# Turning update factors and probabilities on VectorE, GpSimd and ScalarE, and queueing VectorE's side work behind the weight splits, in a hybrid attention/RWKV layer on one core

## The chip, the core and the metric

One core of a Trainium2 chip runs the whole layer in one launch. The metric is the device time of that launch in microseconds (us). Its engines are TensorE (PE in the profile; its weight loads are PEld), VectorE (DVE), ScalarE (ACT), GpSimd (POOL) and SyncE (SP), which here issues nearly all DMAs. Each engine works through its own list of instructions in order; an instruction that waits holds back all behind it on that engine.

## What is computed

The reference, cut to what matters here (shapes: 256 tokens, width 4096, 16 FoX heads of 128, 32 RWKV heads of 64, chunks of 64):

```python
def reference(x, w_in, f_bias, mu_shift, w0, w_up, a0, a_up, k_k, k_a, r_k, gn_gain, gn_bias, w_out, ln_gain, ln_bias):
    proj = jnp.einsum('bsd,dc->bsc', x, w_in)
    ...
    fox_out = _fox_attention(fq, fk, fv, log_f)
    ...
    rw = rw + (rw_prev - rw) * mu_shift
    r, kr, vr, wd, ad = jnp.split(rw, _split_points(IN_SIZES[4:9]), axis=-1)
    w_raw = -jax.nn.softplus(-(w0 + jnp.tanh(wd) @ w_up)) - 0.5
    decay = jnp.exp(-jnp.exp(w_raw))
    a = jax.nn.sigmoid(a0 + ad @ a_up)
    ...
    y = _rwkv7_scan(rh, decay, kh, vh, -kk, kk * ah)
    ...
    h = jnp.concatenate([fox_out, rwkv_out], axis=-1) * jax.nn.silu(z)
    out = jnp.einsum('bsc,cd->bsd', h, w_out)
    return _layernorm(ALPHA * x + out, ln_gain, ln_bias, LN_EPS)
```

In `_fox_attention` a block of 128 queries takes the softmax of its logits (a score plus a decay bias, causal) and multiplies the probabilities with the values. `_rwkv7_scan` is the recurrence `S = S diag(w) + (S a) b^T + v k^T; y = S r`, frame by frame.

## The kernel before

**Main work.** The input projection runs as 8 head pairs (n) of 4 blocks (b) of 512 columns, each over 4096 rows in 16 pieces (q) of 128x1024 weights; the output projection as 8 blocks of the same pieces. A piece is called w{n}_{b}_{q} (w4_3_13 is piece 13 of block 3 of pair 4; the profile leaves the pair and block out and calls it w_13). Every weight is split in a high and a low part: ScalarE writes the high one (L141), VectorE the rest (L142, the "split"). A piece then takes 12 matmuls of 512 columns on TensorE (L147 to L149; L880 to L882 for the output), of which four read the low part, the first of them third in order. `weights` keeps three pieces traced ahead: while TensorE works on piece q, the split last traced (`latest`) is that of piece q+2. The low parts have three buffers, so the split of piece q+2 can start when TensorE has ended piece q-1; the high parts have four.

**Side work.** All the rest (the heads' attention and recurrence, and the way from projection to heads) is cut into generators. `slot()` is called after each 6 matmuls, twice a piece, and moves every generator one `yield` on; so `wait(W[...])` puts steps a number of slots apart. `W` is a table of such distances. What a slot traces comes after the main work traced before it in priority, but a scheduler orders each engine's list: an instruction whose inputs are there may go ahead of earlier traced ones that still wait. Only the side work inside `with behind(...)` (the SV steps of pair 0 and the first softmax step of heads 0 and 1) is tied to come after the split last traced.

- `prepare` and `front` (L419, L471) make, for each 128 channels i, the decays. They split the low-rank weights upt into uph (ScalarE) and upl (VectorE, L424); one slot later six small matmuls (lp, L430 to L432) read both.
- `rwkv` (L522) treats a pair in chunks of 64. It makes the gram products gp, scales the update factors BK on GpSimd (L538), and turns BK for all four chunks with TensorE into tp (L571) and copies it to BKt with ScalarE (L572). Then it solves a triangular system row by row: 31 rows, each one multiply (L600) and one reduction (L603) on VectorE, one row a slot. Then come vm (L615) and eight SV steps (L623), and, some 12 slots on, the state update: rh, up and sp on TensorE with copies between. sp (L687) reads BKt, for chunks 0 to 2 only. The solved rows go through DRAM (td, T) to the matmuls qt (L638).
- `fox` (L734) does one head: the scores fsp (L743, L744), the softmax steps lg (L750 to L754, the exponential on ScalarE), three transposes of the probabilities on TensorE (fpt, L758), a ScalarE copy to pT (L760), and `W["fo"]` = 3 slots later the product with the values fop (L764, L765). Head 2n's softmax falls in block 3 of pair n, head 2n+1's in the pair after.
- `unload` turns each finished block on VectorE (bk, L809) and sends it through DRAM.

Of the kernel before, what the change touches and what calls it, by code (L numbers as in the profile page):

```python
# [10 lines left out]
F32 = mybir.dt.float32  # L11
# [3 lines left out]
ALU = mybir.AluOpType  # L15
AX = mybir.AxisListType

P = 128
# [4 lines left out]
C = 64  # L23
NCH = S // C
HD = 64
LORA = 96
NF = 16
# [17 lines left out]
BEHIND = 13  # L45
W = {"fo": 3, "vs": 2, "np": 4, "gp": 5, "tp": 4, "d1": 8, "d2": 12, "xp": 3, "fs": 4, "fp": 5}
NB = D // OB
# [3 lines left out]
B = 32  # L51
# [33 lines left out]
def layer(ctx: ExitStack, tc: tile.TileContext, xt, xtok, w_main, w_lora, w_first, muv, w_o, up, par, mulora, fbias, lng, lnb, cst, out):  # L85
    nc = tc.nc
# [8 lines left out]
    def pst(name):  # L95
        return ps.tile([P, 512], F32, tag="ps", name=name)
# [34 lines left out]
    ident = cs[:, C_ID : C_ID + P]  # L131
# [4 lines left out]
    latest = [None]  # L136
# [50 lines left out]

    def behind(first):
        return tc.issue_after(latest[0].ins) if first else nullcontext()

    sides = []
# [8 lines left out]
    def slot():  # L200
        for g in list(sides):
            try:
                next(g)
            except StopIteration:
                sides.remove(g)

# [56 lines left out]
    rp = mid.enter_context(tc.tile_pool(name="rp", bufs=1))  # L263
# [65 lines left out]
    ct = const.tile([P, 2 * NF], F32, name="ct")  # L329
# [69 lines left out]
    def flat(t):  # L399
        return t.rearrange("p a b -> p (a b)")  # L400
# [121 lines left out]
    def rwkv(n):  # L522
# [4 lines left out]
        lc, BK, LT, bon = q["lc"], q["BK"], q["lt"], q["bon"]  # L527
# [3 lines left out]
        for u in range(2):  # L531
            for c in range(NCH):
                for j in range(2):
                    h = HALF[j]
# [31 lines left out]
        yield from wait(W["tp"])  # L566
        BKt = rp.tile([P, 2, NCH, P], F32, tag="shl", name=f"BKt{n}")
        for u in range(2):
            tp = pst(f"tp{n}_{u}")
            for c in range(NCH):  # L570
                nc.tensor.transpose(tp[:, c * P : (c + 1) * P], BK[:, u, c, :], ident)  # L571
            nc.scalar.copy(flat(BKt[:, u]), tp)  # L572
        yield from wait(W["d1"])

# [42 lines left out]
        for j in range(2):  # L617
            o = HALF[1 - j]
            for c in range(2):
                h = HALF[c]  # L620
                for a in range(2):
                    with behind(not n):
                        nc.vector.scalar_tensor_tensor(  # L623
                            SV[j][o, :, 2 * a + c, :], vm[h, a, :, j].unsqueeze(2).to_broadcast([C, 2, HD]), -1.0 / HD, vt[h, a, :, j, :], ALU.mult, ALU.add
                        )
            tc.keep_in_program_order(nc.scalar.copy(UV[j][o], SV[j][o]))
            nc.gpsimd.memset(SV[j][HALF[j], :, 0, :], 0.0)
# [106 lines left out]
    def fox(i, q, k, vt):  # L734
# [13 lines left out]
        for m, blk in enumerate((slice(0, 1), slice(1, 3))):  # L748
            with behind(i < 2):
                nc.vector.scalar_tensor_tensor(lg[:, blk, :], spv[:, blk, :], ct[:, m * NF + i : m * NF + i + 1], nb[:, blk, :], ALU.add, ALU.add)  # L750
            nc.vector.tensor_reduce(st[:, m : m + 1], lg[:, blk, :], AX.XY, ALU.max, negate=True)
            nc.scalar.activation(lg[:, blk, :], lg[:, blk, :], AF.Exp, bias=st[:, m : m + 1], accum_out=st[:, 2 + m : 3 + m])
            nc.vector.reciprocal(st[:, 4 + m : 5 + m], st[:, 2 + m : 3 + m])
            nc.vector.tensor_scalar(lg[:, blk, :], lg[:, blk, :], st[:, 4 + m : 5 + m], None, ALU.mult)  # L754
        yield from wait(W["fp"])
        pt = pst(f"fpt{i}")
        for m in range(3):
            nc.tensor.transpose(pt[:, m * P : (m + 1) * P], lg[:, m, :], ident)  # L758
        pT = rp.tile([P, 3 * P], F32, tag="nb", name=f"pT{i}")
        nc.scalar.copy(pT, pt[:, : 3 * P])  # L760
        yield from wait(W["fo"])
# [145 lines left out]
    vt = None  # L907
# [210 lines left out]
```

## Time and profile before

| | |
|---|---|
| median of 3 runs | 1936.33 us (1934.52 to 1938.71) |
| profiled execution, its own time | 1935.4 us |
| its span | 1933.6 us |
| granted TensorE clock | 0.999 |
| TensorE transposes of BK (L571) | 64 in 8 groups |
| TensorE transposes of probabilities (L758) | 48 in 16 groups |
| VectorE splits of main pieces (L142) | 31 of each of the 16 numbers q, 1.21 to 1.33 us each |
| GpSimd copies (L462) | 96 |

How to read it: a row of the timeline has start, duration, engine, line, operation, the tiles written and read (out<-in) and their shapes; a row of the groups has count, then busy us and mean ns of one, then idle time before it and what ended it; a row of one line has minimum, median and maximum in ns. A row of the waits has who waited, for whom, the total in us, how many times and the longest. The ends of matmuls are modelled, so their distance from start to start tells more than their duration.

### The profile page before, as it was taken

The numbers are of one execution on the slowest core, as the hardware profiler recorded it, in microseconds if no ns is written. First come the engines' busy times: TensorE is split into PE (matmuls) and PEld (weight loads), VectorE is DVE, ScalarE is ACT, GpSimd is POOL, SyncE is SP. The second block draws the span as 40 slices with busy tenths as digits, with TensorE's granted clock in tenths as the row PEclk, the third lists the DMA queues.
The fourth block names the chain that finished last, engine by engine and source line by source line (L and its number), as shares of the span: only waits on it lengthen the run. The fifth ranks groups of instructions, "written<-read, shape, count | busy, mean of one in ns | idle before, by whom it ended". The sixth has DMA issues, their size and how long they took to land.

```text
span 1933.6 us, 27829 instructions
## 1 busy us (share of the span) xinstructions
PE 1916.5 (99%) x9897; PEld 1594.4 (82%) x9897; DVE 1363.2 (71%) x2323; ACT 963.5 (50%) x1447; POOL 124.2 (6%) x207
## 2 busy tenths in 40 slices
PE   9999999999999999999999999999999999999998
PEld 9888788788888888888888888888888888888886
DVE  6677768857786778677857795779577856755555
ACT  6554464455545644464456444645464554443332
POOL 0020002000200020002000200020001001000000
PEclk9999999999999999999999999999999999999999
DMA  9577667767686778677867677777777777766564
GB/s 343 152 237 229 200 199 215 223 201 216 206 238 198 214 214 236 195 216 211 233 195 220 211 228 202 217 212 220 215 210 221 238 278 242 251 199 197 186 204 166
DMA packets 269391, 420.04 MB, mean 217 GB/s; under 512 B 142338, under 2 KB 169364, under 8 KB 269252
## 3 DMA queue, kind: packets, MB, share of 16 engines
q1 hardware_dynamic: 268820, 417.58, 70.7%
q8 instruction: 77, 1.26, 0.3%
q10 hardware_dynamic: 432, 0.69, 0.1%
q14 instruction: 62, 0.51, 0.1%
HBM read 388.55 MB, written 29.64 MB: 216 GB/s over the span
## 4 chain that ended last, share of the span: by engine, by line
PE 95%; DVE 3%; DMA 1%; issue 0%; ACT 0%; SPq 0%; DVEq 0%; ACTq 0%
PE acc L147 23%; PE acc L149 23%; PE acc L148 23%; PE oacc L880 6%; PE oacc L881 6%; PE oacc L882 6%; PE gp L536 1%; PE rh L647 1%; PE up L678 1%; PE sp L687 1%; PE accl L149 0%; PE accl L148 0%; PE accl L147 0%; PE yp L709 0%; DVE prod L600 0%; DVE xc L603 0%
## 5 line engine op out<-in xcount | busy, mean ns | idle before, releaser
L603 DVE TENSOR_REDUCE xc<-prod 128x8 f32<-128x16 f32 (+30 forms) x248 | 73.1, 295 | 6.5
L600 DVE TENSOR_TENSOR prod<-Nb,xc 128x8 f32<-128x8 f32 (+30 forms) x248 | 71.4, 288 | 6.5 <-DMA Nb<-nd 0.4
L142 DVE TENSOR_TENSOR w_6l<-w,w_6h 128x1024 fp32r<-128x1024 f32 x31 | 37.9, 1222 | 37.5 <-ACT w_6h L141 25.4
L142 DVE TENSOR_TENSOR w_5l<-w,w_5h 128x1024 fp32r<-128x1024 f32 x31 | 41.3, 1333 | 29.5 <-PE acc L149 23.2
L142 DVE TENSOR_TENSOR w_12l<-w,w_12h 128x1024 fp32r<-128x1024 f32 x31 | 38.0, 1227 | 33.5 <-issue 13.8
L740 POOL TENSOR_SCALAR_AFFINE_SELECT nb<-nb 128x128 f32<-128x128 f32 x32 | 15.8, 498 | 705.2 <-DMA nb<-ncd 514.0
L141 ACT CAST w_12h<-w 128x1024 fp32r<-128x1024 f32 x31 | 32.5, 1050 | 48.4 <-DMA w<-in_w_main_dram 19.1
L142 DVE TENSOR_TENSOR w_10l<-w,w_10h 128x1024 fp32r<-128x1024 f32 x31 | 37.9, 1223 | 24.0 <-issue 17.9
L142 DVE TENSOR_TENSOR w_7l<-w,w_7h 128x1024 fp32r<-128x1024 f32 x31 | 37.9, 1222 | 22.1 <-PE acc L149 15.3
L141 ACT CAST w_13h<-w 128x1024 fp32r<-128x1024 f32 x31 | 32.5, 1049 | 40.7 <-PE acc L148 29.0
L141 ACT CAST w_5h<-w 128x1024 fp32r<-128x1024 f32 x31 | 32.6, 1051 | 40.1 <-PE acc L148 37.1
L142 DVE TENSOR_TENSOR w_11l<-w,w_11h 128x1024 fp32r<-128x1024 f32 x31 | 37.9, 1221 | 19.7 <-PE acc L149 19.7
L142 DVE TENSOR_TENSOR w_8l<-w,w_8h 128x1024 fp32r<-128x1024 f32 x31 | 37.8, 1219 | 19.7 <-PE acc L149 15.4
L149 PE MATMUL acc<-w_7l,x 128*128 128x512 f32 x124 | 47.7, 394 | 3.9 <-DVE w_7l L142 3.8
L147 PE MATMUL acc<-w_8h,x 128*128 128x512 f32 x124 | 50.8, 410 | 0.0
L147 PE MATMUL acc<-w_7h,x 128*128 128x512 f32 x124 | 49.9, 403 | 0.2 <-ACT w_7h L141 0.2
L142 DVE TENSOR_TENSOR w_13l<-w,w_13h 128x1024 fp32r<-128x1024 f32 x31 | 37.9, 1222 | 17.2 <-issue 8.3
L147 PE MATMUL acc<-w_3h,x 128*128 128x512 f32 x124 | 49.9, 403 | 0.0
L147 PE MATMUL acc<-w_5h,x 128*128 128x512 f32 x124 | 49.8, 402 | 0.0
L147 PE MATMUL acc<-w_11h,x 128*128 128x512 f32 x124 | 49.8, 402 | 0.0
L147 PE MATMUL acc<-w_15h,x 128*128 128x512 f32 x124 | 49.6, 400 | 0.0
L147 PE MATMUL acc<-w_9h,x 128*128 128x512 f32 x124 | 49.2, 397 | 0.0
(813 smaller groups left out, 6518.7 us busy)
## 6 DMA issues: line engine op xcount, KB each, us to landing
w<-in_w_main_dram SPq DMA_DIRECT2D x496, 512.0 KB, 3.9
wo<-in_w_o_dram SPq DMA_DIRECT2D x128, 512.0 KB, 4.4
bt<-bk SPq DMA_DIRECT2D x88, 128.0 KB, 4.2
Nb<-nd SPq DMA_DIRECT2D x16, 512.0 KB, 4.7
hd<-hl SPq DMA_DIRECT2D x29, 256.0 KB, 3.5
h<-hd SPq DMA_DIRECT2D x29, 256.0 KB, 6.5
wr<-in_w_first_dram SPq DMA_DIRECT2D x15, 384.0 KB, 6.4
lr<-in_w_lora_dram SPq DMA_DIRECT2D x14, 336.0 KB, 5.2
```

The source lines that it names most:

```text
L141: nc.scalar.copy(hi[:, :n], src[:, :n])
L142: latest[0] = nc.vector.tensor_tensor(lo[:, :n], src[:, :n], hi[:, :n].bitcast(F32), ALU.subtract)
L147: nc.tensor.matmul(acc[:, :n], xs[k][:, 0, tt], hi[:, o : o + n], start=(k == 0), stop=False)
L148: nc.tensor.matmul(acc[:, :n], xs[k][:, 1, tt], hi[:, o : o + n], start=False, stop=False)
L149: nc.tensor.matmul(acc[:, :n], xs[k][:, 0, tt], lo[:, o : o + n], start=False, stop=(k == KT - 1))
L536: nc.tensor.matmul(o, BK[h, u, c, :], lt[j][h, u, c], start=True, stop=True)
L600: first = nc.vector.tensor_tensor(prod[:, :, :, s + 1 :], nb[:, :, s : s + 1, s + 1 :].to_broadcast([P, 2, NJ, w]), xc[:, :, :, s + 1 :], ...
L603: nc.vector.tensor_reduce(xc[:, :, :, s : s + 1], prod[:, :, :, s:], AX.X, ALU.add)
L647: nc.tensor.matmul(rh[:, u * P : (u + 1) * P], LT[:, u, c, 0:P], flat(SVt[:, u, c]), start=True, stop=True)
L880: nc.tensor.matmul(acc, ht[k][:, 0, tt], hi, start=(k == 0), stop=False)
L881: nc.tensor.matmul(acc, ht[k][:, 1, tt], hi, start=False, stop=False)
L882: nc.tensor.matmul(acc, ht[k][:, 0, tt], lo, start=False, stop=(k == KT - 1))
```

## The change

Three things are done:

1. `slot()` traces all side work inside `tc.issue_after(latest[0].ins)`: every VectorE instruction of side work is tied to come after the weight split last traced. `behind` goes, being covered.
2. The update factors: VectorE turns BK in place, in blocks of 32x32, for chunks 0 to 2 (two transposes of 128x384 a pair); GpSimd moves the 16 blocks to their places in BKt (16 copies of 32 partitions by 192), with two more `yield`s between them. tp, its 8 transposes on TensorE and the two ScalarE copies go.
3. The probabilities: VectorE turns lg in place (one transpose of 128x384 a head); 16 copies of 32 partitions by 96, half by GpSimd and half by ScalarE, put the blocks into pT. fpt with its 3 transposes and the wide ScalarE copy go. `W["fo"]` is 7 instead of 3.

```diff
-W = {"fo": 3, "vs": 2, "np": 4, "gp": 5, "tp": 4, "d1": 8, "d2": 12, "xp": 3, "fs": 4, "fp": 5}
+W = {"fo": 7, "vs": 2, "np": 4, "gp": 5, "tp": 4, "d1": 8, "d2": 12, "xp": 3, "fs": 4, "fp": 5}
...
-    def behind(first):
-        return tc.issue_after(latest[0].ins) if first else nullcontext()
...
     def slot():
-        for g in list(sides):
-            try:
-                next(g)
-            except StopIteration:
-                sides.remove(g)
+        with tc.issue_after(latest[0].ins):
+            for g in list(sides):
+                try:
+                    next(g)
+                except StopIteration:
+                    sides.remove(g)
...
         yield from wait(W["tp"])
-        BKt = rp.tile([P, 2, NCH, P], F32, tag="shl", name=f"BKt{n}")
+        BKt = rp.tile([P, 2, NCH - 1, P], F32, tag="shl", name=f"BKt{n}")
         for u in range(2):
-            tp = pst(f"tp{n}_{u}")
-            for c in range(NCH):
-                nc.tensor.transpose(tp[:, c * P : (c + 1) * P], BK[:, u, c, :], ident)
-            nc.scalar.copy(flat(BKt[:, u]), tp)
+            v = flat(BK[:, u, : NCH - 1, :])
+            nc.vector.transpose(v, v)
+        for a in range(4):
+            for b in range(4):
+                nc.gpsimd.tensor_copy(BKt[B * b : B * (b + 1), :, :, B * a : B * (a + 1)], BK[B * a : B * (a + 1), :, : NCH - 1, B * b : B * (b + 1)])
+            if a % 2:
+                yield
         yield from wait(W["d1"])
...
         yield from wait(W["fp"])
-        pt = pst(f"fpt{i}")
-        for m in range(3):
-            nc.tensor.transpose(pt[:, m * P : (m + 1) * P], lg[:, m, :], ident)
-        pT = rp.tile([P, 3 * P], F32, tag="nb", name=f"pT{i}")
-        nc.scalar.copy(pT, pt[:, : 3 * P])
+        nc.vector.transpose(flat(lg), flat(lg))
+        pT = rp.tile([P, 3, P], F32, tag="nb", name=f"pT{i}")
+        for a in range(4):
+            for b in range(4):
+                (nc.gpsimd.tensor_copy if b % 2 else nc.scalar.copy)(pT[B * b : B * (b + 1), :, B * a : B * (a + 1)], lg[B * a : B * (a + 1), :, B * b : B * (b + 1)])
+        pT = flat(pT)
         yield from wait(W["fo"])
```

How this moves instructions is seen in the lists of two engines at two places. Line numbers in rows of the changed kernel are its own: as before up to the splits, then two lower (L422 is the old L424); L568 is the new turn of BK and L571 the copies to BKt; one higher in the solve (L601, L604, L616 are the old L600, L603, L615); the same from the SV steps on (L623), one lower from the softmax on (L749 is the old L750), with L755 the turn of the probabilities and L759 the copies to pT; and the same again from the way out of `fox` on (L809).

**VectorE, the end of pair 4's solve.** Names: prod4 and xc4 are the row steps, vm4 and SV4 what follows, w4_3_q the splits. Before, the last rows stand here:

```order
L603 TENSOR_REDUCE xc4_8781<-prod4_8780 128x8
L600 TENSOR_TENSOR prod4_8780<-Nb4_8638,xc4_8781 128x8x30
L603 TENSOR_REDUCE xc4_8781<-prod4_8780 128x8
L600 TENSOR_TENSOR prod4_8780<-Nb4_8638,xc4_8781 128x8x31
L603 TENSOR_REDUCE xc4_8781<-prod4_8780 128x8
L142 TENSOR_TENSOR w4_3_7l_9043<-w4_3_7_8985,w4_3_7h_9042 128x1024
L142 TENSOR_TENSOR w4_3_8l_9066<-w4_3_8_9016,w4_3_8h_9065 128x1024
```

and vm4 with SV4 six splits later:

```order
L142 TENSOR_TENSOR w4_3_12l_9184<-w4_3_12_9122,w4_3_12h_9183 128x1024
L753 RECIPROCAL fst8_9140<-fst8_9140 128x1
L615 TENSOR_REDUCE vm4_9205<-vs4_8507 128x8
L754 TENSOR_SCALAR lg8_9139<-lg8_9139,fst8_9140 128x256
L623 SCALAR_TENSOR_TENSOR SV4_8657<-vm4_9205,vs4_8507 64x2x64 x8
L142 TENSOR_TENSOR w4_3_13l_9234<-w4_3_13_9159,w4_3_13h_9233 128x1024
```

With the change all of it stands behind the split of w4_3_13 (the row step of width 29 just behind that split is left out):

```order
L616 TENSOR_REDUCE vm4_9367<-vs4_8627 128x8
L604 TENSOR_REDUCE xc4_8925<-prod4_8924 128x8
L623 SCALAR_TENSOR_TENSOR SV4_8777<-vm4_9367,vs4_8627 64x2x64
L601 TENSOR_TENSOR prod4_8924<-Nb4_8758,xc4_8925 128x8x30
L623 SCALAR_TENSOR_TENSOR SV4_8777<-vm4_9367,vs4_8627 64x2x64
L604 TENSOR_REDUCE xc4_8925<-prod4_8924 128x8
L623 SCALAR_TENSOR_TENSOR SV4_8777<-vm4_9367,vs4_8627 64x2x64
L601 TENSOR_TENSOR prod4_8924<-Nb4_8758,xc4_8925 128x8x31
L623 SCALAR_TENSOR_TENSOR SV4_8777<-vm4_9367,vs4_8627 64x2x64
L604 TENSOR_REDUCE xc4_8925<-prod4_8924 128x8
L623 SCALAR_TENSOR_TENSOR SV4_8777<-vm4_9367,vs4_8627 64x2x64 x4
L142 TENSOR_TENSOR w4_3_14l_9390<-w4_3_14_9303,w4_3_14h_9389 128x1024
```

The last rows moved back by six splits, vm4 and SV4 by one, and both now lie between two neighbouring splits.

**VectorE and TensorE, the low part upl10 of pair 5's low-rank weights.** Before, VectorE has it behind the split of w4_1_14, a pair ahead of its use:

```order
L142 TENSOR_TENSOR w4_1_14l_8403<-w4_1_14_8344,w4_1_14h_8402 128x1024
L518 SCALAR_TENSOR_TENSOR BK4_8238<-s1_8_8226,prm_73,ae8_8149 64x4x64 x2
L438 TENSOR_SCALAR tw9_8396<-tw9_8396 128x256
L424 TENSOR_TENSOR upl10_9875<-upt10_8381,uph10_9873 96x256
L440 SCALAR_TENSOR_TENSOR L9_8413<-cs_72,tw9_8396 128x256
```

With the change it is the last side step behind the split of w5_1_3 (lg9 is head 9's probabilities, hl19 and h19 a gated output, bk5_0 a finished block):

```order
L142 TENSOR_TENSOR w5_1_2l_9995<-w5_1_2_9926,w5_1_2h_9994 128x1024
L378 SCALAR_TENSOR_TENSOR h19_9980<-post4_9863,zr9_9784 128x256
L142 TENSOR_TENSOR w5_1_3l_10013<-w5_1_3_9959,w5_1_3h_10012 128x1024
L382 TENSOR_TENSOR hl19_9982<-h19_9980,hl19_9982 128x256
L755 STREAM_TRANSPOSE lg9_9947<-lg9_9947 128x384
L809 STREAM_TRANSPOSE bk5_0_9985<-bk5_0_9985 128x512 x2
L422 TENSOR_TENSOR upl10_10051<-upt10_8501,uph10_10049 96x256
L142 TENSOR_TENSOR w5_1_4l_10058<-w5_1_4_9992,w5_1_4h_10057 128x1024
```

and TensorE reads it near the end of piece w5_1_2:

```order
L148 MATMUL acc5_1_1_9991<-w5_1_2h_9994,x5_288 128x512
L430 MATMUL lp10_10067<-lr_840,upl10_10051 128x256
L428 MATMUL lp10_10067<-lr_840,uph10_10049 128x256
L429 MATMUL lp10_10067<-lr_840,uph10_10049 128x256
L430 MATMUL lp10_10067<-lr_840,upl10_10051 128x256
L149 MATMUL acc5_1_1_9991<-w5_1_2l_9995,x5_288 128x512
```

Before, all six lp10 matmuls stand together in the middle of w5_1_1, with upl10 a pair old; now the first two (L428, L429, on uph10) stand in the middle of w5_1_2 and the rest behind five more main matmuls.

More of the change, by code (lines that the diff above doesn't have):

```diff
@@ L1 @@
 import math
-from contextlib import ExitStack, nullcontext
+from contextlib import ExitStack
 import numpy as np
@@ L621, in rwkv @@
                 for a in range(2):
[L622 to L625, printed above, removed]
+                    nc.vector.scalar_tensor_tensor(
+                        SV[j][o, :, 2 * a + c, :], vm[h, a, :, j].unsqueeze(2).to_broadcast([C, 2, HD]), -1.0 / HD, vt[h, a, :, j, :], ALU.mult, ALU.add
+                    )
             tc.keep_in_program_order(nc.scalar.copy(UV[j][o], SV[j][o]))
@@ L748, in fox @@
         for m, blk in enumerate((slice(0, 1), slice(1, 3))):
-            with behind(i < 2):
-                nc.vector.scalar_tensor_tensor(lg[:, blk, :], spv[:, blk, :], ct[:, m * NF + i : m * NF + i + 1], nb[:, blk, :], ALU.add, ALU.add)
+            nc.vector.scalar_tensor_tensor(lg[:, blk, :], spv[:, blk, :], ct[:, m * NF + i : m * NF + i + 1], nb[:, blk, :], ALU.add, ALU.add)
             nc.vector.tensor_reduce(st[:, m : m + 1], lg[:, blk, :], AX.XY, ALU.max, negate=True)
```

## The prediction, made before the changed kernel ran

> **What bounds the kernel now.** I read the busy shares first, then the chain that ended last, then what TensorE (PE) waited for.
>
> ```profile
> span 1933.6 us, 27829 instructions
> PE 1916.5 (99%) x9897; PEld 1594.4 (82%) x9897; DVE 1363.2 (71%) x2323; ACT 963.5 (50%) x1447; POOL 124.2 (6%) x207
> PE 95%; DVE 3%; DMA 1%; issue 0%; ACT 0%; SPq 0%; DVEq 0%; ACTq 0%
> ```
>
> TensorE is busy for all but 17 us and carries 95% of the chain. So a microsecond taken from its list is a microsecond of the span, as long as nothing it reads comes later than before; and each late operand costs its full lateness. VectorE (DVE) at 71% has room on average, but that is an average over stretches that differ.
>
> ```profile
> PE acc L149 <- DVE w_7l L142: 3.8, 2, 3.4
> PE acc L149 <- DVE w_1l L142: 0.6, 1, 0.6
> PE qt L638 <- DMA T<-td: 0.4, 1, 0.4
> ```
>
> Of what TensorE waited for in the main loop, 4.4 us go to two weight splits that came late: VectorE had them behind side work.
>
> **What is taken off TensorE.** Pieces without side work show its pace, and two groups of transposes show what they cost in it.
>
> ```profile
> 743.57 0.39 PE L147 MATMUL acc<-w_0h,x 128*128 128x512 f32 x1
> 757.16 0.39 PE L147 MATMUL acc<-w_5h,x 128*128 128x512 f32 x1
> ...
> 526.40 0.39 PE L149 MATMUL acc<-w_6l,x 128*128 128x512 f32 x1
> 526.63 1.04 PE L571 MATMUL tp<-cs,BK 128*128 128x128 f32 x8
> 527.43 0.48 PE L147 MATMUL acc<-w_7h,x 128*128 128x512 f32 x1
> 527.75 0.40 PE L148 MATMUL acc<-w_7h,x 128*128 128x512 f32 x1
> ...
> 582.41 0.39 PE L149 MATMUL acc<-w_10l,x 128*128 128x512 f32 x1
> 582.64 0.49 PE L758 MATMUL fpt<-cs,lg 128*128 128x128 f32 x3
> 582.89 0.48 PE L147 MATMUL acc<-w_11h,x 128*128 128x512 f32 x1
> 583.20 0.39 PE L148 MATMUL acc<-w_11h,x 128*128 128x512 f32 x1
> ```
>
> Five pieces take 13.59 us: 2.72 each, 0.227 per matmul. From 526.40 to 527.75 lie 1.35 us where two steps of 0.227 would be 0.45, so eight factor transposes cost 0.90; eight pairs make 7.2. From 582.41 to 583.20 lie 0.79, so three probability transposes cost 0.34; sixteen heads make 5.4. **Removed: 12.6 us.**
>
> **What takes their place, and its cover.** VectorE gets 32 transposes of 128x384. The bounds are 0.44 and 0.70 (rows L466 and L809 of this kernel are 256 and 512 wide; the latter stands below); I take 0.55: 17.6 us in all, in its 570 idle ones. GpSimd (POOL) gets 256 copies of 32 partitions, ScalarE (ACT) 128.
>
> ```profile
> L572 ACT COPY BKt<-tp x16: 576/586/594, 150.0 to 1486.3; 128x512 f32<-128x512 f32 x16
> L760 ACT COPY pT<-fpt x16: 464/469/481, 197.3 to 1585.2; 128x384 f32<-128x384 f32 x16
> ...
> L462 POOL COPY hr<-hr x64: 193/376/1492, 98.6 to 1461.7; 32x16 f32<-32x16 f32 x64
> 502.20 3.08 POOL L462 COPY hr<-hr 32x16 f32<-32x16 f32 x4 [0.50 <-DVE hr L459]
> 504.01 1.23 DVE L142 TENSOR_TENSOR w_1l<-w,w_1h 128x1024 fp32r<-128x1024 f32 x1
> ...
> 609.58 0.52 PE sp L687 x4
> ```
>
> ScalarE loses 16.9 us and gains 128 copies that cost at most the 0.469 of the wider copy: at most 3.8 us a head while it is half idle, so nothing on TensorE. A GpSimd copy costs 0.19 alone and up to 1.49; the nearest case is four in 3.08 us beside VectorE splits, 0.77 each. The sixteen of the factors then take 12 us; they start near the old transposes (526.6) and the first reader sp runs at 609.6: 80 us of cover, nothing to pay. The eight of a probability tile take 6 us. For the even head of pair 4 VectorE's transpose ends about 9.7 us after TensorE starts w4_3_8 (three splits, eight row steps, softmax, the transpose: prices below), so they end at 15.9; fop, now four slots later, stands in the middle of w4_3_14, at 18.4. Nothing to pay, with 2.5 us to spare.
>
> GpSimd and VectorE share a port, and here one rule speaks against the change. The SBUF page, "SBUF — State Buffer", section "SBUF: two separate sides", in the Trainium skill says the pair is an exclusive lock: whichever of a GpSimd op or a VectorE op with two SBUF inputs starts first holds it throughout, and the other fully blocks.
>
> ```profile
> 514.68 2.15 POOL L541 TENSOR_TENSOR vs<-vs,muv 128x512 f32<-128x512 f32 x1
> 513.80 1.88 DVE L142 TENSOR_TENSOR w_5l<-w,w_5h 128x1024 fp32r<-128x1024 f32 x1 [1.49 <-PE acc L149]
> ```
>
> Beside a two-input GpSimd op a split took 1.88 instead of 1.22, so there VectorE pays. Beside the four copies it took 1.23 and the copies waited. I go by the copies: no price on VectorE; the other case is a rival.
>
> **What the new order on VectorE removes and adds.** All side work now queues behind the latest traced split. That removes the 4.4 us: the two late splits go ahead of the work that held them. But side work that ran ahead in idle time can no longer do so, and it bunches.
>
> ```profile
> 371.69 0.38 DVE L600 TENSOR_TENSOR prod<-Nb,xc 128x216 f32<-128x216 f32 x1
> 375.15 0.42 DVE L600 TENSOR_TENSOR prod<-Nb,xc 128x248 f32<-128x248 f32 x1
> 375.94 0.68 DVE L615 TENSOR_REDUCE vm<-vs 128x8 f32<-128x512 f32 x1
> 376.65 2.00 DVE L623 SCALAR_TENSOR_TENSOR SV<-vm,vs 64x128 f32<-64x128 f32 x8
> 378.68 1.23 DVE L142 TENSOR_TENSOR w_7l<-w,w_7h 128x1024 fp32r<-128x1024 f32 x1
> 379.83 1.22 DVE L142 TENSOR_TENSOR w_8l<-w,w_8h 128x1024 fp32r<-128x1024 f32 x1
> ...
> L750 DVE SCALAR_TENSOR_TENSOR lg<-fsp,ct,nb 128x128 f32<-128x128 f32 (+1 forms) x32 | 12.4, 412 | 5.2 <-PE fsp L744 5.0
> L751 DVE TENSOR_REDUCE fst<-lg 128x1 f32<-128x128 f32 (+1 forms) x32 | 10.2, 340 | 0.0
> L754 DVE TENSOR_SCALAR lg<-lg,fst 128x128 f32<-128x128 f32 (+1 forms) x32 | 9.7, 305 | 0.1
> L753 DVE RECIPROCAL fst<-fst 128x1 f32<-128x1 f32 x32 | 4.7, 150 | 0.8 <-ACT lg L752 0.8
> L384 DVE TENSOR_TENSOR hl<-h,hl 128x256 fp32r<-128x256 f32 x32 | 13.5, 421 | 8.7 <-ACT hl L383 8.4
> L466 DVE STREAM_TRANSPOSE post<-hry 128x512 f32<-128x512 f32 x8 | 5.7, 713 | 0.3
> L809 DVE STREAM_TRANSPOSE bk<-bk 128x512 f32<-128x512 f32 x44 | 31.0, 704 | 6.6 <-ACT bk L920 4.2 <-ACT bk L918 2.2
> L424 DVE TENSOR_TENSOR upl<-upt,uph 96x256 fp32r<-96x256 f32 x16 | 6.6, 411 | 6.6 <-PE fpt L758 5.5 <-ACT uph L422 1.1
> ...
> L743 PE MATMUL fsp<-fk,fq x32: 271/274/377, 185.4 to 1575.3; 128*128 128x128 f32 x32
> L744 PE MATMUL fsp<-fk,fq x32: 379/380/382, 185.6 to 1575.7; 128*128 128x256 f32 x32
> ```
>
> First place: the end of the solve's rows. In pairs 2 to 7 the last rows, vm and the eight SV steps used to lie pieces apart; now they lie between the splits of w4_3_13 and w4_3_14. From the split of w4_3_10, whose buffer comes free when TensorE starts w4_3_8, VectorE has four splits (4.9), fifteen row steps of 0.36 to 0.42 (5.9), the softmax of head 8 (0.82 + 0.68 + 0.61 + 0.30 = 2.4), its transpose (0.55), vm (0.68) and SV (2.0 to 2.3), then the split itself (1.2): 17.9 us. TensorE reaches that low part after six pieces, fsp (0.65) and two matmuls: 17.4. A sum of durations runs long, for neighbours that don't depend on each other overlap (378.68 + 1.23 is past 379.83); the head's exponentials on ScalarE may add as much. Bounds 0 and 1.1; I take 0.5, six times: **+3.0**.
>
> Second place: upl10. It was computed a pair early; now it stands last of its bunch, and lp10 stands where the old lead isn't there. The clock of this bunch starts when fsp9 ends on TensorE, for the first lg step needs it. From there to upl10: softmax 2.4, the group norm's transpose 0.71 and small reciprocal 0.15, eight steps of 128x256 at 0.42 (3.4), three splits (3.7), the new transpose 0.55, two bk transposes (1.4), upl 0.41: 12.7. TensorE, from the same instant: three pieces (8.2), eleven matmuls of the fourth (2.5), two small lp ones (0.2): 10.9. Late by 1.8; overlap takes some 0.3 to 0.4. Bounds 0.9 and 2.2; I take 1.5 for pairs 3 to 7, and 0.9 for pair 2 where the bunch is shorter: **+8.4**. Behind upl10 on VectorE stands only the split of w5_1_4, not needed for two more pieces.
>
> Third: the first pair's rows end in the same bunch as before, one row step later than now: it cost 0.6; by the same sum 1.0 more: **+1.6**.
>
> **Sum.** -12.6 - 4.4 + 3.0 + 8.4 + 1.6 = -4.0 us on an execution of 1935.4 us (span 1933.6 and 1.8 around it): 1931.4. The median shown is 0.9 above that execution, so I forecast **1932 us**.
>
> **The rivals.** *The new waits come in full*: 1.1 x 6 + 2.0 x 5 + 1.5 + 2.1 = 20, so +3: 1939. For it: the same bunch recurs in each pair. Against it: the overlap. *No new waits*: VectorE's overlap eats the 0.5 and half the 1.8, leaving some 4 us: 1923. For it: 570 idle us; against it: the second shortfall is far beyond the overlap. *Slower, by late GpSimd copies*: fop of the even heads in the row stretch, priced above with 2.5 us to spare, decides from 1.1 us per copy; at 1.4 (near the 1.49 seen) it is 2.4 late, seven times: +17, 1949. For it: VectorE works without pause there; against it: the median copy took 0.376. *Slower, by VectorE blocked*: in each stretch eight copies of 0.28 (0.19 and 80 more elements) hold two-input steps; half of them met make 1.1 us in each of some eleven full stretches: +12, 1944. That is what the Trainium skill's lock rule (page and section above) would make here; the split beside GpSimd's two-input op agrees with it, the one beside its copies does not.
>
> **How the numbers follow.** Forecast 0.45 (its own range 1926 to 1938), full waits 0.20, no new waits 0.14, late copies 0.13, blocked VectorE 0.08. What this measurement can tell from no change is about 0.2%, 3.9 us: 1932.5 to 1940.2 is "same". Faster: 0.28 of the forecast's 0.45, all of no new waits, 0.02 else: 0.44. Same: 0.17 and 0.11 of the full waits: 0.28. Slower: the rest, 0.28. The range 1921 to 1944 leaves out the late copies' upper part and a little below.
>
> **What would show it.** The transposes tp and fpt gone from TensorE, 112 matmuls fewer. In TensorE's waits: a new line lp <- DVE upl of 5 to 11 us in about six times; acc <- DVE w_14l (about six times, up to 1.1 each); w_7l's 3.4 us gone. GpSimd busy about 300 us, and no wait fop <- POOL pT; if that line is there, copies are late. Splits still 1.22 us beside copies; if they lengthen, the port decides. Wrong altogether if lp doesn't wait, or if TensorE's pace of 0.227 changes.

## The result, and the profile after

The changed kernel takes 1922.66 us (median of 4 runs, 1921.70 to 1924.20), the kernel before 1935.87 on the same chip (4 runs): a ratio of 0.9930, 95% interval 0.9917 to 0.9942, or 13.2 us less. The forecast was 1932 us and "faster"; the sign is right, the gain was put at a third of its size. The profiled execution took 1921.7 us.

From the page of the changed kernel, the lines that answer to those quoted of before (span, busy shares, chain by engine):

```profile
span 1919.5 us, 27983 instructions
PE 1906.1 (99%) x9785; PEld 1583.1 (82%) x9785; DVE 1375.6 (72%) x2355; ACT 987.3 (51%) x1543; POOL 259.1 (13%) x463
PE 96%; DVE 2%; DMA 1%; ACT 1%; issue 0%; SPq 0%; DVEq 0%; ACTq 0%
```

The span is 14.1 us shorter: TensorE is busy 10.4 less (112 matmuls fewer) and idle 13.4 instead of 17.1. The waits of TensorE's matmuls that the profile lists sum to 10.1 us before and 7.1 after, so 3 of the 14 us are waits and some 11 come off its list of work. What it waits for in the main loop (waiter, for whom, total us, times, longest):

```profile
PE acc L149 <- DVE w_2l L142: 1.4, 1, 1.4
PE acc L149 <- DVE w_10l L142: 1.0, 1, 1.0
PE up L678 <- ACT R L650: 0.9, 1, 0.9
PE acc L147 <- ACT w_11h L141: 0.4, 1, 0.4
```

The long wait for w_7l is gone, and there is no line of a matmul that waits for upl, for w_14l or for pT. The forecast had 13.0 us of new waits; there are 3.7. What is left is single events: w_2l is the end of pair 0's rows, the third place of the forecast; w_10l, w_11h and R were not foreseen.

The new instructions (count, then shortest, median and longest in ns):

```profile
L755 DVE STREAM_TRANSPOSE lg<-lg x16: 567/571/578, 196.0 to 1569.9; 128x384 f32<-128x384 f32 x16
L568 DVE STREAM_TRANSPOSE BK<-BK x16: 527/546/564, 150.3 to 1474.7; 128x384 f32<-128x384 f32 x16
L759 POOL COPY pT<-lg x128: 258/264/1492, 196.6 to 1573.7; 32x96 f32<-32x96 f32 x128
L571 POOL COPY BKt<-BK x128: 338/343/2312, 151.5 to 1485.1; 32x192 f32<-32x192 f32 x128
```

The turns cost the 0.55 that was put in. The copies' median is less than half of the 0.77 that was put in.

**The place where upl was to be 1.5 us late.** VectorE from the first softmax step of head 9 (its wait for fsp ends there) to upl, in pair 5; start and duration in us, some rows left out:

```profile
1023.11 0.35 DVE L749 SCALAR_TENSOR_TENSOR lg<-fsp,ct,nb 128x128 f32<-128x128 f32 x1 [0.40 <-PE fsp L744]
1023.38 0.24 DVE L721 RECIPROCAL hry<-hry 128x16 f32<-128x16 f32 x1
...
1025.67 1.22 DVE L142 TENSOR_TENSOR w_1l<-w,w_1h 128x1024 fp32r<-128x1024 f32 x1
1026.81 0.42 DVE L378 SCALAR_TENSOR_TENSOR h<-post,zr 128x256 f32<-128x256 f32 x1
...
1031.34 0.41 DVE L382 TENSOR_TENSOR hl<-h,hl 128x256 fp32r<-128x256 f32 x1
1031.67 0.57 DVE L755 STREAM_TRANSPOSE lg<-lg 128x384 f32<-128x384 f32 x1
1032.17 1.26 DVE L809 STREAM_TRANSPOSE bk<-bk 128x512 f32<-128x512 f32 x2
1033.35 0.40 DVE L422 TENSOR_TENSOR upl<-upt,uph 96x256 fp32r<-96x256 f32 x1
```

and TensorE there:

```profile
1033.63 0.39 PE L148 MATMUL acc<-w_2h,x 128*128 128x512 f32 x1
1033.85 0.34 PE L430 MATMUL lp<-lr,upl 96*128 96x256 f32 x1
```

The 25 instructions are those that the forecast listed, and their durations sum to 12.5 us (forecast: 12.7). But upl ends at 1033.75, 10.64 after the first start. Each record reaches past the next one's start: 0.35 after 1023.11 is 0.08 past 1023.38; 1.22 after 1025.67 is 0.08 past 1026.81; 0.57 after 1031.67 is 0.07 past 1032.17. Over the 24 neighbours that makes 1.9 us. lp starts 0.10 after upl's end and 0.22 behind the matmul ahead of it, TensorE's usual pace: no wait. But it is close. In the answer on the tile upl, under those who waited for it, stands the weight load of lp (PEld; us in all, times):

```profile
  PEld lp L430: 1.3, 6
```

Six loads, one in each of pairs 2 to 7, waited 0.2 us each for upl, where the forecast had looked for a wait. They did so while the matmul ahead was running, so no matmul came late.

**The place where w_14l was to be 0.5 us late.** The bunch at the rows' end, in pair 4, from the split of w_10 to that of w_14, and the first matmul that reads the latter (the last rows lie seven splits further back than before, behind w_13 instead of w_6):

```profile
949.28 1.22 DVE L142 TENSOR_TENSOR w_10l<-w,w_10h 128x1024 fp32r<-128x1024 f32 x1
964.86 1.22 DVE L142 TENSOR_TENSOR w_14l<-w,w_14h 128x1024 fp32r<-128x1024 f32 x1
966.45 0.39 PE L149 MATMUL acc<-w_14l,x 128*128 128x512 f32 x1
```

From 949.28 to the split's end at 966.08 lie 16.8 us, and TensorE reads it 0.36 later.

### The profile page after: what moved, and what is told of

Same layout as the page of the kernel before. It is cut to its first block, busy times and chain, and to the rows that moved or that the text cites. A ratio compares the mean times of both kernels' runs of the same rounds, so it can differ in the third digit from the quotient of the medians.

```text
span 1919.5 us, 27983 instructions
## 1 busy us (share of the span) xinstructions
PE 1906.1 (99%) x9785; PEld 1583.1 (82%) x9785; DVE 1375.6 (72%) x2355; ACT 987.3 (51%) x1543; POOL 259.1 (13%) x463
## 4 chain that ended last, share of the span: by engine, by line
PE 96%; DVE 2%; DMA 1%; ACT 1%; issue 0%; SPq 0%; DVEq 0%; ACTq 0%
PE acc L147 24%; PE acc L149 23%; PE acc L148 23%; PE oacc L882 6%; PE oacc L880 6%; PE oacc L881 6%; PE gp L534 1%; PE rh L647 1%; PE up L678 1%; PE sp L687 1%; PE accl L149 1%; PE accl L147 1%; DMA w<-in_w_main_dram 1%; PE accl L148 0%; PE yp L709 0%
## 5 line engine op out<-in xcount | busy, mean ns | idle before, releaser
L759 POOL COPY pT<-lg 32x96 f32<-32x96 f32 x128 | 59.6, 466 | 406.7 <-DVE lg L755 402.0
L571 POOL COPY BKt<-BK 32x192 f32<-32x192 f32 x128 | 76.8, 600 | 55.2 <-DVE BK L568 50.2
L604 DVE TENSOR_REDUCE xc<-prod 128x8 f32<-128x16 f32 (+30 forms) x248 | 72.2, 291 | 5.5
L601 DVE TENSOR_TENSOR prod<-Nb,xc 128x8 f32<-128x8 f32 (+30 forms) x248 | 72.1, 291 | 3.6
L142 DVE TENSOR_TENSOR w_14l<-w,w_14h 128x1024 fp32r<-128x1024 f32 x31 | 38.0, 1225 | 39.4 <-ACT w_14h L141 33.3
L142 DVE TENSOR_TENSOR w_5l<-w,w_5h 128x1024 fp32r<-128x1024 f32 x31 | 39.7, 1282 | 16.8 <-PE acc L149 10.5
L141 ACT CAST w_9h<-w 128x1024 fp32r<-128x1024 f32 x31 | 32.5, 1050 | 35.9 <-PE acc L148 25.5
L142 DVE TENSOR_TENSOR w_3l<-w,w_3h 128x1024 fp32r<-128x1024 f32 x31 | 37.9, 1222 | 18.0 <-ACT w_3h L141 10.2
L149 PE MATMUL acc<-w_2l,x 128*128 128x512 f32 x124 | 48.4, 391 | 1.4 <-DVE w_2l L142 1.4
```

The costliest lines, as they stand in the source:

```text
L141: nc.scalar.copy(hi[:, :n], src[:, :n])
L142: latest[0] = nc.vector.tensor_tensor(lo[:, :n], src[:, :n], hi[:, :n].bitcast(F32), ALU.subtract)
L149: nc.tensor.matmul(acc[:, :n], xs[k][:, 0, tt], lo[:, o : o + n], start=False, stop=(k == KT - 1))
L571: nc.gpsimd.tensor_copy(BKt[B * b : B * (b + 1), :, :, B * a : B * (a + 1)], BK[B * a : B * (a + 1), :, : NCH - 1, B * b : B * (b + 1)])
L601: first = nc.vector.tensor_tensor(prod[:, :, :, s + 1 :], nb[:, :, s : s + 1, s + 1 :].to_broadcast([P, 2, NJ, w]), xc[:, :, :, s + 1 :], ...
L604: nc.vector.tensor_reduce(xc[:, :, :, s : s + 1], prod[:, :, :, s:], AX.X, ALU.add)
```

## Experiments

All twelve were compared with the kernel before on their own chip; the changed kernel's ratio, for comparison, is 0.9930. The groups of four ran on three chips, so differences between ratios of two groups are good to some 0.15%, 3 us.

| kernel | median us (runs) | before | ratio, 95% interval |
|---|---|---|---|
| order_alone | 1937.3 (11) | 1937.6 | 0.9999 (0.9990 to 1.0007) |
| moves_alone | 1946.6 (5) | 1937.6 | 1.0050 (1.0037 to 1.0062) |
| fo3 | 1948.1 (5) | 1937.6 | 1.0062 (1.0049 to 1.0076) |
| prob_back | 1926.5 (5) | 1937.6 | 0.9947 (0.9934 to 0.9959) |
| prob_old_order | 1932.0 (9) | 1937.3 | 0.9977 (0.9967 to 0.9986) |
| fact_back | 1935.8 (11) | 1937.3 | 0.9996 (0.9987 to 1.0005) |
| turn2_even | 1924.4 (5) | 1937.3 | 0.9935 (0.9923 to 0.9948) |
| sv_spread | 1921.2 (4) | 1937.3 | 0.9917 (0.9903 to 0.9930) |
| turn2_odd | 1925.1 (6) | 1937.1 | 0.9942 (0.9929 to 0.9954) |
| pool16 | 1930.7 (5) | 1937.1 | 0.9966 (0.9954 to 0.9978) |
| late_tie | 1922.5 (5) | 1937.1 | 0.9923 (0.9911 to 0.9934) |
| fact_back_fo9 | 1927.3 (6) | 1937.1 | 0.9955 (0.9942 to 0.9969) |

### Order and moves, each alone

order_alone is the kernel before with the first part of the change (`behind` then does nothing):

```diff
     def slot():
-        for g in list(sides):
+        with tc.issue_after(latest[0].ins):
+            for g in list(sides):
```

> The kernel before, with only the first part of the change: all side work is traced behind the weight split last traced; factors and probabilities are still turned by TensorE, and the product with the values is 3 slots away. Theory A (neighbouring VectorE work overlaps, so the new bunches cost little): the waits for w_7l and w_1l go (-4.4), and what came in their place in the changed kernel's trace stays, w_2l 1.4, w_10l 1.0, R 0.9, w_11h 0.4 (+3.7): about 1935 us, between 1933 and 1937, and no wait lp <- VectorE upl. Rival B (the forecast's sum, in which durations hardly overlap): -4.4 and some 9 to 13 of new waits: 1940 to 1945, with lp <- upl among the waits.

1937.3 us against 1937.6, no change, and no wait for upl: theory A and not rival B, though not by the waits that A named. Those for w_7l go, the one for w_1l (0.6) stays, and others come (w_10l 2.7, qt 1.6).

moves_alone is the changed kernel without that part, with `behind` restored:

```diff
     def slot():
-        with tc.issue_after(latest[0].ins):
-            for g in list(sides):
+        for g in list(sides):
...
-                    nc.vector.scalar_tensor_tensor(
+                    with behind(not n):
+                        nc.vector.scalar_tensor_tensor(
```

> The changed kernel without the first part: side work may run ahead of the splits as before; factors and probabilities are turned by VectorE and moved by GpSimd and ScalarE, 7 slots to the product with the values. Theory A (the gain is the 112 matmuls taken from TensorE, 12.6 us, and does not hang on the order): 1936 - 12.6 = 1923 us, between 1921 and 1925, with the waits for w_7l and w_1l (about 4 us) still there. Rival C (the order is what lets TensorE keep the gain: VectorE's 32 new turns of 0.55 would else go ahead of splits and make these late): 1928 us or more, with more than 8 us of waits for low parts.

1946.6 us: 9 slower than before, where the gain of 12.6 would have made it faster. Theory A falls. Its first wait of TensorE, and VectorE between the splits of w_6 and w_7 in block 3 of pair 2 (first moves_alone, then the kernel before; count, busy us, mean ns):

```profile
PE acc L149 <- DVE w_7l L142: 16.1, 6, 6.9
```

```profile
L606 DVE TENSOR_REDUCE xc<-prod 128x8 f32<-128x208 f32 (+6 forms) x7 | 2.8, 398 | 0.2
L603 DVE TENSOR_TENSOR prod<-Nb,xc 128x200 f32<-128x200 f32 (+6 forms) x7 | 2.7, 391 | 0.2
```

```profile
L603 DVE TENSOR_REDUCE xc<-prod 128x8 f32<-128x224 f32 (+4 forms) x5 | 2.0, 404 | 0.1
L600 DVE TENSOR_TENSOR prod<-Nb,xc 128x224 f32<-128x224 f32 (+3 forms) x4 | 1.6, 405 | 0.1
```

In the old order the scheduler lets the last row steps run ahead of the split of w_7: nine before, which left that split 0.2 to 0.8 us to spare in four of pairs 2 to 6 (in pair 4 it came 0.3 late), and fourteen here, 2 us more, so that it comes some 1.8 us late in each of the five (9.2 in all) and 6.9 late in pair 1. That is not all of it: TensorE's granted clock is 0.50 for 3.4 us behind each of four waits of 1.3 to 2.2 us and for 4.9 us behind the wait of 6.9. Half of these 18.5 us is lost, 9 us, in the profiled execution, which is 3.4 above the median. With 16 us more of waits than before (26.2 against 10.1) and some 11 less work that makes 14, where the span (1948.2) is 14.6 longer than before.

prob_old_order asks which of the moves does it: it keeps the old order and moves the probabilities alone, leaving the factors on TensorE (moves_alone, but with these lines as they were):

```diff
-            v = flat(BK[:, u, : NCH - 1, :])
-            nc.vector.transpose(v, v)
+            tp = pst(f"tp{n}_{u}")
+            for c in range(NCH):
+                nc.tensor.transpose(tp[:, c * P : (c + 1) * P], BK[:, u, c, :], ident)
+            nc.scalar.copy(flat(BKt[:, u]), tp)
```

> The kernel before with the probabilities alone moved (turned by VectorE, copied by GpSimd and ScalarE, 7 slots to the product with the values); the factors stay on TensorE and side work may run ahead of the splits. In this kernel's list nine row steps stand between the splits of w_6 and w_7 in block 3 of a pair, as in the kernel before; without the first part of the change but with the factors moved too it was fourteen. Theory F (in the old order it is only the factors' two added steps, which let five more row steps run ahead of w_7, that make TensorE wait; the VectorE turns themselves do not): waits for w_7l as before, about 4 us, and the 5.4 of the probabilities gained: about 1931 to 1932 us. Rival G (any VectorE work added in the old order makes the splits late, since w_7l had only 0.1 to 0.8 us to spare): waits for w_7l of 8 us or more, 1937 us or more.

1932.0 us, 5.3 less than before on its chip (4.5 by the ratio), with w_7l at 4.3: theory F. The probabilities' 5.4 is gained in the old order as far as these runs can tell; what spoils it is the factors' part. That its two more `yield`s do it, by putting the rows two slots back, is argued from the fourteen row steps; no run has the `yield`s without the turns and the copies. Tied behind the splits, the rows can't run ahead. So the order, worth nothing alone, is what the factors' move needs.

### The distance to the product with the values

```diff
-W = {"fo": 7, ...
+W = {"fo": 3, ...
```

> The changed kernel with the product with the values 3 slots behind the probabilities' copies instead of 7. Theory A (the copies take some 16 x 0.34 / 2 = 2.7 us, as the median copy of the changed kernel says, and 3 slots are 4.1 us): no wait for pT to speak of, 1923 us, the same as the changed kernel within 2. Rival D (copies are late, as a copy of 0.77 or more would make them: 8 x 0.77 = 6.2 us and VectorE's turn queued behind splits): a wait of TensorE for pT of 1 to 5 us in most heads, 1935 us or more.

1948.1 us: theory A falls, and rival D holds in eight of the sixteen heads. The waits, then GpSimd and TensorE at an odd head:

```profile
PE fop L764 <- POOL pT L759: 14.7, 8, 2.1
```

```profile
850.42 4.54 POOL L759 COPY pT<-lg 32x96 f32<-32x96 f32 x8 [11.30 <-DVE lg L755]
```

```profile
852.49 0.40 PE L149 MATMUL acc<-w_2l,x 128*128 128x512 f32 x1
855.01 0.70 PE L764 MATMUL fop<-pT,vt 128*128 128x256 f32 x2 [2.11 <-POOL pT L759]
855.54 0.38 PE L765 MATMUL fop<-pT,vt 128*128 128x128 f32 x2
855.68 0.48 PE L147 MATMUL acc<-w_3h,x 128*128 128x512 f32 x1
...
856.64 0.63 PE L147 MATMUL acc<-w_3h,x 128*128 128x512 f32 x1
857.07 0.63 PE L148 MATMUL acc<-w_3h,x 128*128 128x512 f32 x1
```

The eight copies take 4.54 us here, 0.57 each, against the 0.34 that I had taken. The waits sum to 14.7 but the span is 23.3 longer than the changed kernel's. The rest is in the last two rows: matmuls that follow each other by 0.23 elsewhere do so by 0.43. The granted clock there, from the view by stretches (the last three numbers are the clock, the DMA share and GB/s), and then behind the 6.9 us wait of moves_alone:

```profile
855.70:859.60 3.90, 3.90 (x13) 3.10 (x12) 1.88 (x4) 2.27 (x7) 0.00 (x0) 0.57 0.84 132
```

```profile
387.40:392.10 4.70, 4.67 (x11) 3.71 (x12) 3.03 (x4) 4.19 (x6) 0.00 (x0) 0.50 0.66 183
```

A stretch of 3.90 at 0.57 costs 1.7 us. There are four of them in this execution, 6.8 us: behind three of its five waits of 2.1 us and behind one of 1.85. With 14.7 that is 21.5 of the 23.3.

### The factors, and the probabilities, back on TensorE

prob_back is the changed kernel with the old lines of the probabilities:

```diff
-        nc.vector.transpose(flat(lg), flat(lg))
+        pt = pst(f"fpt{i}")
+        for m in range(3):
+            nc.tensor.transpose(pt[:, m * P : (m + 1) * P], lg[:, m, :], ident)
...
+        nc.scalar.copy(pT, pt[:, : 3 * P])
```

> The changed kernel with the probabilities turned by TensorE again (48 matmuls and a wide ScalarE copy back; the factors stay with VectorE and GpSimd). Theory A (each transpose costs TensorE what the pieces beside it show, 0.34 us a head): 5.4 us more than the changed kernel, 1928 us. Rival E (the transposes fill TensorE time that is lost anyway, or what they need from VectorE costs as much as they save): less than 2 us more.

1926.5 us; its span of 1924.9 is 5.4 longer than the changed kernel's. The medians differ by 3.9, the ratios by 3.3 us: theory A within the error. Of the 5.4, 1.2 are waits at other places (w_10l 2.3 instead of 1.0, above all); the list itself grows by some 4.

fact_back puts the old lines of the factors back in the changed kernel, as in prob_old_order; the two added `yield`s go with the copies.

> The changed kernel with the factors turned by TensorE again (64 matmuls and two wide ScalarE copies a pair back, the two added steps gone); the probabilities stay moved and side work stays behind the splits. By the transposes' price in TensorE's list, 0.90 for eight: 7.2 us more than the changed kernel, 1930 us. By the runs so far (the order alone 0, the probabilities within the new order 4 us of the changed kernel's 14): 9 to 10 us more, 1932 us. If the factors on VectorE cost the row bunch what they save, less than 3 us more.

1935.8 us, 13 more: beyond all three. A new wait says where:

```profile
PE fop L761 <- POOL pT L756: 6.8, 5, 1.4
```

```profile
970.80 5.92 POOL L756 COPY pT<-lg 32x96 f32<-32x96 f32 x8 [65.25 <-DVE lg L752]
```

(At the same place in the changed kernel:)

```profile
958.25 3.51 POOL L759 COPY pT<-lg 32x96 f32<-32x96 f32 x8 [42.92 <-DVE lg L755]
```

Without the two `yield`s the rows' end comes a piece earlier and the even head's turn stands behind the SV steps. Its copies then run beside four splits in a row: the first four take 1.1 to 1.2 each and the others 0.26, a mean of 0.74 instead of 0.44. This is the forecast's "late GpSimd copies" in a neighbouring kernel. The price per copy is near its 0.77; they are late because the turn is. Two more slots to the product test that:

```diff
-W = {"fo": 7, ...
+W = {"fo": 9, ...
```

> The changed kernel with the factors turned by TensorE again, and the product with the values 9 instead of 7 slots behind the probabilities, so that the waits for pT of five even heads (6.8 us with 7 slots) have 1.4 to 2.7 us more. Theory A (what the factors' move is worth in TensorE's list is 0.90 for eight transposes, 7.2 in all, and the rest of the 13 us that their return cost was the wait for pT): no wait for pT, 1936 - 6.8 = 1929 us. Rival K (the wait for pT only hides another): 1933 us or more.

1927.3 us, no wait for pT. What the factors' move brings in the new order is then 4.6 us by the medians and by the spans (1924.1 against 1919.5), where eight transposes eight times are 7.2. The listed waits sum to the same 7.1 in both executions. The price is there in its trace, 0.89 at each of the eight groups of transposes; what offsets 2.5 of it stands elsewhere in TensorE's list. Some 1.0 is the start: in the changed kernel's execution the matmuls follow each other at half the pace until 6.9 us, in this one only until the first wait ends at 4.8. Another 0.6 is the lp matmuls, which take that much longer in the changed kernel's list. The rest stays open.

### How near the bunches are to a wait

turn2_even and turn2_odd turn the probabilities of the even or of the odd heads three times:

```diff
-        nc.vector.transpose(flat(lg), flat(lg))
+        for _ in range(3 if i % 2 == 0 else 1):
+            nc.vector.transpose(flat(lg), flat(lg))
```

> The changed kernel with the probabilities of every even head turned three times instead of once (two turns in place undo each other), so VectorE has two more instructions of 0.57 in the bunch at the end of the rows; all else stands as it was. In the changed kernel the split of w_14 ended 0.36 us before TensorE read it, in five pairs. Theory A (a bunch costs TensorE only what goes past that spare time): 1.0 to 1.14 more on VectorE, less 0.36: a wait for w_14l of 0.65 to 0.8 in five pairs, 3 to 4 us, and nothing more at other places: 1926 us. The forecast's sum (0.5 late already): 1.5 each. Rival H (spare time at the other splits takes it up): no wait, 1923 us.

1924.4 us, 1 to 2 more than the changed kernel; one wait for w_14l, of 0.7. The split of w_14 still comes in time in four of pairs 2 to 6, with 0.1 to spare instead of 0.36: the scheduler put two row steps more ahead of the split of w_13, whose spare time fell from 4.1 to 2.6 us. Rival H, nearly.

> The changed kernel with the probabilities of every odd head turned three times instead of once, so VectorE has two more instructions of 0.57 ahead of upl in the bunch in which the forecast looked for its largest wait. In this kernel's list the scheduler has put the lp matmuls on upl eight main matmuls (1.8 us) further back, and two row-independent turns stand between the two bk turns. Theory A (neighbours on VectorE overlap, the bunch takes about 2 us less than the sum of its durations, and the reader stands where the scheduler expects upl): no wait for upl, 1923 us, within 1 of the changed kernel. The forecast's sum (1.8 late in the changed kernel's list): 1.14 more work against 1.8 more of TensorE, so still 1.1 late in five pairs: 5 to 6 us more, 1928 us, with a wait lp <- upl.

1925.1 us. No wait for upl but one of 0.2: the forecast's sum falls here too. The 1.3 us that fop waits for pT in five odd heads is new, since the last turn comes later and the eight copies behind it take 6.0 us.

pool16 has GpSimd make all sixteen copies of a tile:

```diff
-                (nc.gpsimd.tensor_copy if b % 2 else nc.scalar.copy)(
+                nc.gpsimd.tensor_copy(
```

> The changed kernel with all sixteen copies of a probability tile on GpSimd (ScalarE makes none): 128 more GpSimd copies. Theory A (a copy takes 0.34 alone, and up to 0.9 where VectorE's splits stand beside it; the even heads' tiles have some 4 us to spare, since eight copies took 3.5): 16 x 0.45 to 0.9 = 7 to 14 us instead of 3.5, so a wait of TensorE for pT of 0 to 6 us in the even heads: 1923 to 1950 us, and if the wait is there it is in the even heads and worth what the copies' length says. VectorE's splits stay at 1.22 (the copies wait, not VectorE). Rival J (VectorE is held by GpSimd's copies): splits beside copies of 1.4 us or more, and waits for w_13l to w_15l.

```profile
PE fop L764 <- POOL pT L759: 4.6, 8, 1.5
PE acc L149 <- DVE w_10l L142: 1.5, 1, 1.5
```

1930.7 us, 8 more. pT is late in eight heads: the even ones of pairs 0 and 1 (0.8 and 1.5) and six odd ones (0.3 to 0.5 each). In the even heads of pairs 2 to 6, where I had looked for it, the sixteen took 6.1 us (0.38 each) and came in time. No split of w_13 to w_15 is waited for, so rival J falls as a price. But VectorE does wait for copies. In the changed kernel, a split that starts just behind a copy of the factors, and one that starts during GpSimd's two-input step on vs:

```profile
911.16 0.34 POOL L571 COPY BKt<-BK 32x192 f32<-32x192 f32 x1
911.17 1.41 DVE L142 TENSOR_TENSOR w_12l<-w,w_12h 128x1024 fp32r<-128x1024 f32 x1 [1.40 <-PE acc L149]
```

```profile
889.59 1.29 POOL L538 TENSOR_TENSOR vs<-vs,bk 128x512 f32<-128x512 f32 x1 [8.88 <-DMA vs<-vd]
889.92 2.04 DVE L142 TENSOR_TENSOR w_5l<-w,w_5h 128x1024 fp32r<-128x1024 f32 x1 [1.50 <-PE acc L149]
```

The first split ends at 912.58 and the copy at 911.50, the second at 891.96 and the GpSimd step at 890.88: both 1.08 later. So a split waits for what is left of the GpSimd instruction. A copy has at most 0.34 left, and the longest split beside one takes 1.41 instead of 1.22, in pool16 too.

### Can it be better?

sv_spread puts a `yield` between the two halves of the SV steps and takes one slot from the wait behind them:

```diff
             nc.gpsimd.memset(SV[j][HALF[j], :, 0, :], 0.0)
+            if not j:
+                yield
-        yield from wait(W["d2"] - 1)
+        yield from wait(W["d2"] - 2)
```

> The changed kernel with the eight SV steps spread over two slots, four each (the wait behind them one slot shorter). In pair 0 four SV steps (1.1 us) leave the stretch ahead of the split of w_2 at 214 us, which came 1.4 late; in pairs 2 to 7 the split of w_14 gets 1.1 us more to spare than its 0.36. Theory A: the wait for w_2l goes and nothing else changes: 1 to 1.5 us less than the changed kernel, about 1921.5 us. Rival I (the 1.4 is not set by that bunch, or it comes back at the next split): within 0.5 us of the changed kernel, with a wait for w_2l or w_3l still there.

1921.2 us, and the wait for w_2l is gone from the trace. By its interval it can't be told from the changed kernel; the missing wait is the evidence. The median is 1.4 less, as theory A said, but the span only 0.8 and the listed waits 0.7, since a wait of 0.6 for R and one of 0.4 for w_9l have come. late_tie also leaves the first 76 slots untied:

```diff
-        with tc.issue_after(latest[0].ins):
+        slots[0] += 1
+        with tc.issue_after(latest[0].ins) if slots[0] > 76 else nullcontext():
```

> The SV steps spread over two slots, as in the run before of that name, and the first 76 slots' side work not tied to the splits (pair 0's preparation may run ahead as in the kernel before). Theory A: the waits for w_9l and w_10l at 97 and 100 us (0.4 and 1.0) go, w_7l's 0.4 at 91 us comes back: about 1 us less than with the SV steps spread alone, 1920 us. Rival: the waits move to another split of that block, no gain.

1922.5 us: the wait for w_9l goes and that for w_10l falls to 0.2, but one for w_8h (0.6) and one for qt (1.2) stand in their place. No gain.

## Why the forecast was right in sign and wrong in size

- **Removed, 12.6: about right.** Between main matmuls the groups of transposes cost some 0.34 and 0.89, in the kernel before as in prob_back and fact_back_fo9; in the kernel before, five of the probabilities' stand beside lp and cost 0.23, which makes 12.0. Of this the kernels give back less: the probabilities 4.5 to 5.3 in the old order and 3.3 to 5.4 in the new one, the factors 4.6.
- **Waits removed, 4.4: right for w_7l's 3.8**; w_1l's 0.6 stays with the order alone. Neither is a gain of its own: the order alone brings nothing.
- **Second place, upl, 8.4: the step that failed.** It said: "overlap takes some 0.3 to 0.4". Overlap took 1.9, on all 24 neighbours and not on a few. The forecast had shown the very row (378.68 + 1.23 is past 379.83, by 0.08) and didn't multiply it. From the start of the bunch VectorE needs 12.5 - 1.9 = 10.6, and TensorE takes 10.7 to lp. The forecast called itself wrong altogether "if lp doesn't wait": no matmul does. The place was right, though: the weight loads wait 0.2 there. The Trainium skill, "VectorE: DVE Perf Modes", section "The DRAIN you can't avoid", says that the next op does not start until the pipe has emptied, which would make the bunch its full sum, but adds that an op that is not held starts earlier. The records here, which overlap, agree with the addition.
- **First place, the rows' end, 3.0: the same step.** It said 17.9 against 17.4, and let overlap and VectorE's pauses cancel. The durations do sum to 17.9 in pair 4, but overlap takes 2.1, and VectorE's pauses give back only 1.0: 16.8 us, with 0.36 to spare. turn2_even shows that it is near the edge and that the scheduler moves with it.
- **Third place, 1.6: right in place**, 1.4 seen as w_2l, where 0.6 (as w_1l) stood before.
- **GpSimd copies, no price: right**, with the 0.77 too high for this order and right for fact_back. The margin is real: fo3, pool16 and fact_back each lose by pT.
- **VectorE not blocked by copies: right in price, wrong in kind.** The forecast went by a split of 1.23 that made the copies wait; when it started, at 504.01, the copy then running had 0.03 us left. That shows one side only. A copy that meets a split ends 0.1 to 0.2 after it (the longest, 2.31, stands beside two), and a split that starts with 0.2 us or more of a copy to go ends 1.08 after the copy. Both agree with the Trainium skill's lock rule ("SBUF — State Buffer", "SBUF: two separate sides"). It costs little because a copy is short: 17 splits of the changed kernel are longer beside copies, by 1.7 us in all, and TensorE waits for none of them.
- **"Each late operand costs its full lateness": too little.** fo3 and moves_alone lost up to 1.7 us more behind a wait of 2, by the clock.
- **What was not seen at all:** the forecast costed the order and the moves apart. They aren't: 0 and +9 make -13 together. It had no rival "the moves without the order".

The rival that came true is "no new waits", 1923 us, which was given 0.14. Its mechanism, the overlap, is what the trace shows. That the 4 us of new waits that it leaves are so near the 3.7 seen is luck: it leaves part of upl's lateness, and 2.3 of the 3.7 stand where the forecast didn't look (w_10l, R, w_11h).

## What to carry to other kernels

A bunch of short independent VectorE instructions is timed by the distances from start to start of such neighbours in the trace, not by the sum of durations: here the sum was 18% too long, 1.9 us, as much as the whole lateness in question (1.8). Before work is put on an engine, look up how long the operands behind it are ready before their reader; where that is less than the work added, the order has to change with the work. A stall of TensorE of 2 us can cost nearly twice its length, so removing one is worth more than the wait that the profile lists.

## What the runs showed of the hardware

- TensorE's granted clock fell to half for 3.4 us (0.50 from 856.24 to 859.65 in fo3) after three of five waits of 2.1 us and one of 1.85 (fo3) and after waits of 1.3, 1.8, 1.9 and 2.2 (moves_alone), and for longer at one of 6.9 (0.50); the matmuls then follow each other by 0.43 instead of 0.23. After a wait of 3.4 in the kernel before it didn't fall. The Trainium skill, "TensorE: Matmul & The Clock Gate", section "Part 1: The HAM clock gate (the "warmup" mystery)", gives the half rate, which agrees, and an idle window of some 3.4 us as its cause; here 1.3 to 2.2 us were enough, in some cases and not in others.
- Neighbouring VectorE records overlap by 0.07 to 0.08 us all through the bunch of upl. Two row steps, of which the second reads the first, stand 0.03 apart; so do SV steps between row steps, which they don't read (in the rows' end of pair 4, an SV step of 960.90 + 0.28 is short of the row step at 961.22). "Independent" alone doesn't make an overlap.
- GpSimd's copies and VectorE's splits shut each other out. A copy of 32x96 takes 0.26 us alone and up to 1.49 beside VectorE: eight of them took 3.51 beside one split and row steps, and 5.92 beside four splits. A split that starts with 0.2 us or more of a GpSimd instruction to go ends 1.08 us after it: it took 1.41 beside a copy of 0.34 and 2.04 beside a step of 1.29.
